# Halved low-part probability products, joined tile-0 scores, split low weight steps and a new rank table in a two-layer hybrid decoder kernel

## The chip, the cores and the metric

The kernel runs on one core of a Trainium2 chip. TensorE (PE) multiplies, VectorE (DVE), ScalarE (ACT) and GpSimd (POOL) do the elementwise work, and SyncE (SP) issues most DMAs. The metric is the device time of one execution in microseconds; smaller is better. Of the kernel before, three timed runs gave 553.5, 553.61 and 555.03 us (median 553.61).

## The reference

The input is 512 tokens of width 1024; two layers follow each other, then a final RMSNorm. In each layer one projection gives the columns of four mixers that work side by side:

```python
h = rmsnorm(x, norm_w)
p = split_cols(h @ w_in)
o_a = dsa_mixer(...)       # ReLU indexer over 8 heads -> top-k keys per query -> softmax attention, 4 heads
o_b = nsa_mixer(...)       # compressed, selected and window branches, each a softmax, sigmoid-gated and added
o_c = shortconv_mixer(...) # 3-wide causal convolution between two gates
o_d = pool_mixer(...)      # causal means over 2/4/8/16 tokens, a small linear map
mixed = concat(silu(gate) * o for each group)
x = x + mixed @ w_out
```

In the indexer, `score = sum_h relu(qi_h . ki) * wi_h`. In each attention, scores go through an exponential, are divided by their row sum, and are multiplied with the values; in mixer B the result is also multiplied by a gate per head and branch. With 512 tokens every block of the selected branch is admissible, so it and the window branch are both plain causal attention, each with its own keys and values.

## The kernel before, in words

Float32 accuracy is had from two fp32r operands: a number is split into a high part (`wh`, `ph`, `hT[0]`, ...) and a low part (`wl`, `pl`, `hT[1]`, ...), and a product is the sum of high*high, high*low and low*high matmuls.

The 512 tokens are four tiles of 128. A layer is: normalisation and transposition of the tiles into `hT`; the projections (token-major ones in `group_a`, `group_idx`, `group_bk`, `group_bq`; channel-major ones by `lin_ch`, with 512 columns a step); the compression of keys and values (`compress`, `compressed`); attention A and B for each tile (`att_a`, `att_b`); convolution and pooling; and the output projection (`out_tile`).

Weights come in parts of 256 rows (`load_w`, line 566). A part is loaded by SP into `st` (four buffers), ACT writes its high part `wh`, and POOL the low part `wl = st - wh`, one subtraction over both 128-row halves `k` of the part. A buffer `st` comes free when `wl` is done. In the first group (`start=True`) DVE makes `wh`, and POOL and DVE take turns with `wl`. `compressed` (line 965) also uses the `st` buffers, for the compression weights, and multiplies them in 64 small matmuls; each is two instructions in a trace.

The indexer (`group_idx`, line 800) does, for tiles 1 to 3 and eight heads each: a matmul into a PSUM bank `s` (there are two), a ReLU by ACT into the SBUF tile `rl` (two buffers), and `acc = rl * wi + acc` by DVE. `topk` then takes the largest values out of `acc` on DVE.

`probs` (line 1005) does for each of the four heads: two matmuls (high and low keys) into a bank `s`; a DVE operation that adds the mask and finds the minimum `mn`; the exponential on ACT into `pb` with the row sum `rs`. Then DVE takes the reciprocal of `rs`, multiplies it with the gate in mixer B (`rs<-rs,gt`), and POOL scales `pb`. `pv` (line 1039) handles 128 keys at a time: four transposes of `pb` into a bank `tr`, the high part `ph` by ACT, the low part `pl` by DVE, and two matmuls with all 512 columns into the bank `pv`. The value operand `vt(k)` has 128 columns: 64 of the high part of V and 64 of the low part; `finish` adds the two halves.

All engines' orders are made before the program runs. Every operation is recorded on a `Tape` (line 521 issues each, so every instruction of a trace has line 521 and rows are told apart by their tiles). `schedule` lists them with a table of costs (`cost`, line 318): on each engine, of the operations that could start within 1 ns of the soonest, the one with the lowest rank goes first. The ranks are the table `RANK`, one number for each recorded stage. `warm` records 40 transposes of the identity that nothing reads.

```python
PE.matmul(po, vt(k), ph, start=first and k == 0, stop=False)      # pv, before
PE.matmul(po, vt(k), pl, start=False, stop=last and k == i)
S.activation(rl[:, :n], ps[:, :n], AF.Relu)                       # group_idx, before
lo(V if start and h % 2 else G, wl[:, :, :n], st[:, :, :n], wh[:, :, :n])   # load_w, before
```

Of the kernel before, what the change touches and what calls it, by code (L numbers as in the profile page):

```python
# [178 lines left out]
class Op:  # L179
    __slots__ = ("eng", "name", "args", "kw", "outs", "ins", "before", "left", "behind", "dur", "occ", "seen",  # L180
                 "tiles", "start", "ready", "num", "locks", "moves", "stage", "rank", "group", "load")


class Engine:
# [43 lines left out]
class Tape:  # L228
# [37 lines left out]
    def record(self, eng, name, args, kw):  # L266
# [11 lines left out]
        op.group = None  # L278
        op.behind = []
# [8 lines left out]
        for views, writes in ((op.ins, False), (op.outs, True)):  # L288
            for v in views:
# [3 lines left out]
                if adds:  # L293
                    op.group = v.tile.groups.setdefault((r0, r1, bits), [])
                    op.group.append(op)
                    for (a, b, _), other in v.tile.groups.items():
                        if other is not op.group and a < r1 and r0 < b:
                            op.before.update((o.num, o) for o in other)
# [19 lines left out]
    def cost(self, op):  # L318
# [9 lines left out]
        if op.name == "dma_start":  # L328
# [3 lines left out]
            op.seen = 2000 + rows * (2.1 + run / 685.0)  # L332
            if op.eng == "ACT" and not any(o.eng == "ACT" for o in self.ops):
                op.occ = 1650
# [59 lines left out]
    def schedule(self):  # L394
# [24 lines left out]
        def earliest(op):  # L419
# [4 lines left out]
            for t in op.tiles:  # L424
# [6 lines left out]
                elif pl.pool.name == "pp":  # L431
                    s = max([s] + [at for other, at in t.used.items() if other != e])
            return s
# [10 lines left out]
        while len(order) < len(ops):  # L444
# [9 lines left out]
            if e == "PE" and last[e] is not None:  # L454
                s = max(s, last[e].start + op.load * (2 if last[e].start < COLD else 1))
# [882 lines left out]
```

## Time and profile before

| what | value |
|---|---|
| median of three timed runs | 553.61 us |
| the profiled execution's own time | 555.73 us |
| its span (first to last instruction) | 554.0 us |
| PE busy | 530.8 us (96%) |
| weight loads (PEld) busy | 457.0 us (82%) |
| DVE busy | 423.3 us (76%) |
| ACT busy | 318.2 us (57%) |
| POOL busy | 297.8 us (54%) |
| DMA | 50.62 MB, mean 91 GB/s |
| mean granted TensorE clock | 0.993 |

A busy share counts an instruction from its start to its end. Matmuls overlap in the pipeline of PE, so the distance between the starts of two steps is what a step costs, not its own duration. PE is nearly always busy here, so a piece of time has to come out of PE's steps, out of the waits between them, or out of the stretches at the two ends where PE has nothing to do. Other engines matter where PE waits for what they make.

### The profile page before, as it was taken

The numbers are of one execution on the slowest core, as the hardware profiler recorded it, in microseconds if no ns is written. First come the engines' busy times: TensorE is split into PE (matmuls) and PEld (weight loads), VectorE is DVE, ScalarE is ACT, GpSimd is POOL, SyncE is SP. The second block draws the span as 40 slices with busy tenths as digits, with TensorE's granted clock in tenths as the row PEclk, the third lists the DMA queues.
The fourth block names the chain that finished last, engine by engine and source line by source line (L and its number), as shares of the span: only waits on it lengthen the run. The fifth ranks groups of instructions, "written<-read, shape, count | busy, mean of one in ns | idle before, by whom it ended". The sixth has DMA issues, their size and how long they took to land.

```text
span 554.0 us, 9676 instructions
## 1 busy us (share of the span) xinstructions
PE 530.8 (96%) x3097; PEld 457.0 (82%) x3097; DVE 423.3 (76%) x1153; ACT 318.2 (57%) x797; POOL 297.8 (54%) x398
## 2 busy tenths in 40 slices
PE   6999999999999999999999999989999999999995
PEld 6999987767887778789999899878778777888995
DVE  4648999999995787843266589998999878797733
ACT  5468855634554676754356686454555665675623
POOL 5655753653446746553665556257455567463632
PEclk9999999999999999999999999989999999999998
DMA  8861222641313111106662333147232202130304
GB/s 270 262 162 30 61 70 72 153 112 31 89 46 87 57 49 46 40 20 203 194 181 66 87 78 88 48 116 177 72 87 57 76 30 59 28 98 10 95 1 151
DMA packets 70098, 50.62 MB, mean 91 GB/s; under 512 B 19224, under 2 KB 64416, under 8 KB 70048
## 3 DMA queue, kind: packets, MB, share of 16 engines
q1 hardware_dynamic: 69888, 49.75, 32.8%
q8 instruction: 24, 0.39, 0.3%
q14 instruction: 26, 0.21, 0.1%
q10 hardware_dynamic: 160, 0.27, 0.1%
HBM read 45.81 MB, written 4.19 MB: 90 GB/s over the span
## 4 chain that ended last, share of the span: by engine, by line
PE 80%; DVE 6%; ACT 5%; DMA 3%; POOL 3%; issue 2%; SPq 0%; POOLq 0%; ACTq 0%; DVEq 0%
PE mm L521 58%; PE tr L521 10%; PE s L521 7%; PE pv L521 5%; POOL wl L521 2%; DMA st<-in_w_in_dram 1%; ACT wh L521 1%; DVE acc L521 1%; DVE pb L521 1%; DMA x<-in_x_dram 1%; DMA st<-in_w_out_dram 1%; DVE om L521 1%; POOL pb L521 1%; ACT rl L521 1%; DVE pl L521 0%
## 5 line engine op out<-in xcount | busy, mean ns | idle before, releaser
L521 POOL TENSOR_TENSOR wl<-st,wh 128x768 fp32r<-128x768 f32 (+4 forms) x94 | 160.2, 1713 | 98.4 <-ACT wh L521 87.2
L521 PE MATMUL mm<-hT,wh 128*128 128x512 f32 x544 | 178.1, 405 | 3.3 <-ACT wh L521 2.7
L521 PEld LDWEIGHTS mm<-hT,wh 128*128 128x128 f32 x544 | 100.4, 190 | 24.3 <-ACT wh L521 4.9
L521 PE MATMUL mm<-wh,hT 128*128 128x360 f32 (+3 forms) x480 | 104.8, 309 | 1.5 <-ACT z L521 0.9
L521 PE MATMUL mm<-hT,wl 128*128 128x512 f32 x272 | 103.6, 401 | 0.0
L521 PE MATMUL mm<-wh,mT 128*128 128x384 f32 (+1 forms) x384 | 92.7, 324 | 0.4 <-DVE x L521 0.4
L521 ACT ACTIVATE wh<-st 128x768 fp32r<-128x768 f32 (+4 forms) x92 | 70.8, 776 | 31.9 <-DMA st<-in_w_in_dram 14.5
L521 POOL TENSOR_SCALAR pb<-pb,rs 128x512 f32<-128x512 f32 (+3 forms) x96 | 55.7, 597 | 52.5 <-DVE rs L521 35.6
L521 PEld LDWEIGHTS mm<-wh,hT 128*128 128x128 f32 x480 | 78.5, 189 | 3.4 <-ACT z L521 1.8
L521 PEld LDWEIGHTS mm<-wh,mT 128*128 128x128 f32 x384 | 66.4, 189 | 3.6 <-ACT wh L521 1.0
L521 PE MATMUL mm<-wl,hT 128*128 128x360 f32 (+3 forms) x240 | 68.3, 306 | 0.0
L521 ACT ACTIVATE pb<-pb,mn 128x128 f32<-128x128 f32 (+3 forms) x96 | 53.5, 558 | 25.2 <-DVE mn L521 24.8
L521 PE MATMUL mm<-wl,mT 128*128 128x384 f32 (+1 forms) x192 | 59.3, 321 | 0.3 <-POOL wl L521 0.3
L521 PEld LDWEIGHTS mm<-hT,wl 128*128 128x128 f32 x272 | 51.0, 189 | 9.5 <-POOL wl L521 0.4
L521 DVE MAX8 m<-acc 128x8 f32<-128x256 f32 (+2 forms) x96 | 51.9, 551 | 0.8
L521 DVE MATCH_REPLACE8 acc<-m,acc 128x384 f32<-128x384 f32 (+2 forms) x96 | 51.8, 541 | 0.1
L521 DVE TENSOR_TENSOR pl<-tr,ph 128x512 fp32r<-128x512 f32 x60 | 40.4, 684 | 9.5 <-ACT ph L521 7.9
L521 ACT ACTIVATE ph<-tr 128x512 fp32r<-128x512 f32 (+1 forms) x68 | 38.2, 592 | 15.0 <-PE tr L521 14.7
L521 PE MATMUL tr<-ident,pb 128*128 128x128 f32 x240 | 43.3, 275 | 2.3 <-POOL pb L521 2.2
L521 PEld LDWEIGHTS mm<-wl,hT 128*128 128x128 f32 x240 | 43.4, 189 | 0.5 <-POOL wl L521 0.2
L521 DVE CUSTOM_DVE_ANT_0 pb<-s,mask 128x128 f32<-128x128 f32 (+3 forms) x72 | 33.1, 461 | 10.0 <-PE s L521 5.2
L521 PEld LDWEIGHTS tr<-ident,pb 128*128 128x128 f32 x240 | 29.9, 140 | 11.4 <-POOL pb L521 6.0
(159 smaller groups left out, 889.0 us busy)
## 6 DMA issues: line engine op xcount, KB each, us to landing
st<-in_w_in_dram SPq DMA_DIRECT2D x104, 128.0 KB, 2.5
st<-in_w_in_dram SPq DMA_DIRECT2D x28, 256.0 KB, 3.2
st<-in_w_out_dram SPq DMA_DIRECT2D x16, 384.0 KB, 3.3
x<-in_x_dram SPq DMA_DIRECT2D x16, 256.0 KB, 5.0
st<-in_w_in_dram SPq DMA_DIRECT2D x8, 320.0 KB, 3.3
st<-in_w_out_dram SPq DMA_DIRECT2D x8, 256.0 KB, 2.7
x1d<-x SPq DMA_DIRECT2D x8, 256.0 KB, 3.8
x<-x1d SPq DMA_DIRECT2D x8, 256.0 KB, 3.4
```

What stands on the lines that cost most here:

```text
L521: getattr(self.engines[op.eng].real, op.name)(*[real(a) for a in op.args], **{k: real(v) for k, v in op.kw.items()})
```

## The change

- In `pv` the low part `pl` meets only the 64 high columns of the values, in two matmuls of 256 columns each; the high part `ph` still meets 128 columns. The product of low part and low values is no longer added (except in the one step of tile 0 of mixer A).
- In mixer B, tile 0, the scores of the window branch, the selected branch and the compressed branch come out of one pair of matmuls per head (`probs_joint`, 2 x 160 columns).
- `load_w` makes `wl` in two subtractions, one for each 128-row half; in the first group POOL takes the first half and DVE the second. ACT's queue issues the first part's DMA.
- The ReLU of the indexer is written back into its PSUM bank; `rl` is gone.
- The gate is no longer multiplied into `rs` on DVE but given to POOL's scaling of `pb` as a second multiplier.
- The tape lets a matmul over a part of a region join that region's accumulation group, prices DMAs otherwise, and counts a step's weight load when it picks the next step. The table `RANK` is a new one.

```diff
 RANK = [
-    583, 29, 585, 581, 518, 0, 283, 160, 177, 3, 101, 151, 129, 145, 507, 102, 0, 68, 584, 582, 532, 0, 74, 105,
+    3, 2, 577, 31, 1, 0, 0, 41, 54, 50, 52, 46, 4, 53, 12, 19, 0, 47, 11, 51, 14, 0, 17, 60, 106, 83, 0, 100, 0,
...
-            op.seen = 2000 + rows * (2.1 + run / 685.0)
+            op.seen = 2000 + rows * (0.56 + run / 437.0)
...
+            if e == "PE" and before is not None:
+                s = max(s, before.start + op.load * (2 if before.start < COLD else 1))
             return s
...
-            if e == "PE" and last[e] is not None:
-                s = max(s, last[e].start + op.load * (2 if last[e].start < COLD else 1))
...
-                SP.dma_start(
+                (S if start and h == 0 else SP).dma_start(
                     st[:, :, o : o + c],
...
-            lo(V if start and h % 2 else G, wl[:, :, :n], st[:, :, :n], wh[:, :, :n])
+            for k in range(2):
+                lo(V if start and k else G, wl[:, k, :n], st[:, k, :n], wh[:, k, :n])
...
-                rl = wk.tile([P, T], F32, name=nm("rl"), tag="rl", bufs=2)
-                S.activation(rl[:, :n], ps[:, :n], AF.Relu)
-                V.scalar_tensor_tensor(a[:, :n], rl[:, :n], wi[i][:, h : h + 1],
+                S.activation(ps[:, :n], ps[:, :n], AF.Relu)
+                V.scalar_tensor_tensor(a[:, :n], ps[:, :n], wi[i][:, h : h + 1],
...
-            if gcol is not None:
-                V.tensor_mul(rs, rs, gate[i][:, :, gcol])
             for h in range(NH):
                 p = pb[h]
-                G.tensor_scalar(p, p, rs[:, h : h + 1], 0.0, op0=OP.mult, op1=OP.add)
+                if gcol is None:
+                    G.tensor_scalar(p, p, rs[:, h : h + 1], 0.0, op0=OP.mult, op1=OP.add)
+                else:
+                    G.tensor_scalar(p, p, rs[:, h : h + 1], gate[i][:, h, gcol : gcol + 1], op0=OP.mult, op1=OP.mult)
...
+                p3 = ps[:, 0:320].rearrange("p (b n) -> p b n", b=2)          # probs_joint, for each head
+                PE.matmul(p3, qT["b", 0][:, h, :], kTB[0][:, :, 0:160], start=True, stop=False)
+                PE.matmul(p3, qT["b", 0][:, h, :], kTB[1][:, :, 0:160], start=False, stop=True)
...
-                PE.matmul(po, vt(k), ph, start=first and k == 0, stop=False)
-                PE.matmul(po, vt(k), pl, start=False, stop=last and k == i)
+
+                end = last and k == i
+                if not end:
+                    PE.matmul(po, vt(k), ph, start=first and k == 0, stop=False)
+                if end and i == 0:
+                    PE.matmul(po, vt(k), pl, start=True, stop=False)
+                else:
+                    for c in (slice(0, T // 2), slice(T // 2, T)):
+                        PE.matmul(po[0:HD, c], vt(k)[:, 0:HD], pl[:, c], start=False, stop=False)
+                if end:
+                    PE.matmul(po, vt(k), ph, start=False, stop=True)
```

The new orders are shown at three places. The first is PE in mixer B of layer 1, where `pl` meets the values (`tr` from `pb` are the transposes, `mm` the projections). Before:

```order
L521 MATMUL mm_1738<-hT_194,wh_1648 128x512
L521 MATMUL s_1787<-kTB_941,qb_1122 128x512
L521 MATMUL s_1787<-kTB_951,qb_1122 128x512
L521 MATMUL pv_1731<-ph_1778,vB_854 128x512
L521 MATMUL pv_1731<-pl_1783,vB_854 128x512
L521 MATMUL tr_1795<-kTB_941,qb_1122 128x32
```

And now:

```order
L529 MATMUL pv_1829<-ph_2015,vB_853 128x512
L529 MATMUL pv_1829<-pl_2018,vB_853 64x256 x2
L529 MATMUL tr_2030<-ident,pb_1869 128x128
L529 MATMUL tr_2030<-ident,pb_1891 128x128
L529 MATMUL pv_1829<-pl_2023,vB_853 64x256
L529 MATMUL pv_1829<-ph_2026,vB_853 128x512
L529 MATMUL tr_2030<-ident,pb_1908 128x128
L529 MATMUL pv_1829<-pl_2023,vB_853 64x256
```

The low product is now two steps, here once in a row (`x2`) and once apart, each behind another kind of step. Of the 116 halves in the program, 56 stand right behind their other half and 15 right behind a transpose.

The second place is PE behind the small compression matmuls of layer 1 (`tr` from `st` and `u`), up to the first projections with weights (`wh_1479` before, `wh_1542` now) whose buffers the compression held. Before:

```order
L521 MATMUL tr_1406<-st_1322,u_106 32x64
L521 MATMUL mm_1452<-hT_194,wh_1114 128x512
L521 MATMUL mm_1452<-hT_212,wh_1114 128x512
L521 MATMUL mm_1452<-hT_194,wl_1156 128x512
...
L521 MATMUL mm_1452<-hT_194,wl_1309 128x512
L521 MATMUL mm_1452<-hT_194,wh_1254 128x512
L521 MATMUL mm_1452<-hT_212,wh_1254 128x512
L521 MATMUL mm_1488<-hT_194,wh_1479 128x512
```

And now:

```order
L529 MATMUL tr_1466<-st_1353,u_152 32x64
L529 MATMUL s_1508<-kTB_98,qb_1310 128x512
L529 MATMUL s_1508<-kTB_104,qb_1310 128x512
L529 MATMUL tr_1518<-ident,pet_901 128x16
L529 MATMUL s_1528<-kTB_98,qb_1310 128x512
L529 MATMUL s_1528<-kTB_104,qb_1310 128x512
L529 MATMUL tr_1547<-ident,zc_1515 128x32
L529 MATMUL mm_1552<-hT_255,wh_1542 128x512
```

Twelve projection and score steps stood between the two before; now four score steps and two small transposes do. In layer 2 it went the other way: two score steps and six transposes stood there before, and eleven projection steps and one transpose do now.

The third place is DVE at the start of the program (`st` are the weight parts, `xn` normalised tiles, `hT` the low part of the transposed ones). Before:

```order
L521 COPY g_col<-tr_125 128x8
L521 SCALAR_TENSOR_TENSOR xn_164<-x_81,ss_133,s_141 128x512
L521 SCALAR_TENSOR_TENSOR xn_174<-x_85,ss_133,s_157 128x512
L521 CAST wh_188<-st_102 128x2x360
L521 SCALAR_TENSOR_TENSOR xn_199<-x_92,ss_155,s_141 128x512
L521 TENSOR_TENSOR hT_212<-tr_181,hT_194 128x4x128
```

And now:

```order
L529 COPY g_col<-tr_122 128x8
L529 CAST wh_168<-st_90 128x2x360
L529 TENSOR_TENSOR wl_175<-st_90,wh_168 128x360
L529 CAST wh_186<-st_102 128x2x360
L529 TENSOR_TENSOR wl_216<-st_102,wh_186 128x360
L529 SCALAR_TENSOR_TENSOR xn_232<-x_81,ss_163,s_139 128x512
L529 SCALAR_TENSOR_TENSOR xn_238<-x_92,ss_163,s_154 128x512
L529 CAST wh_263<-st_165 128x2x360
L529 TENSOR_TENSOR hT_273<-tr_240,hT_255 128x4x128
```

Three weight parts are now cast ahead of the first tile's low part, and the first two ahead of the tile's normalisation. All 40 unread transposes now stand ahead of the first tile's own; before, they were spread between its steps and those of the next tiles.

## Rows read from the trace of the kernel before

**Rows 1.** The page's first part: busy time, share of the span, instructions.

```profile
PE 530.8 (96%) x3097; PEld 457.0 (82%) x3097; DVE 423.3 (76%) x1153; ACT 318.2 (57%) x797; POOL 297.8 (54%) x398
```

**Rows 2.** Timeline, PE near 137 us: start us, us, engine, operation, tiles, shapes, count.

```profile
137.16 0.40 PE L521 MATMUL mm<-hT,wl 128*128 128x512 f32 x1
137.40 0.39 PE L521 MATMUL mm<-hT,wh 128*128 128x512 f32 x1
137.63 0.39 PE L521 MATMUL pv<-pl,vB 128*128 128x512 f32 x1
137.86 0.60 PE L521 MATMUL tr<-ident,es 128*96 128x128 f32 x4
```

**Rows 3.** Waits of the weight loads: total us, times, longest us.

```profile
PEld mm L521 <- ACT wh L521: 6.4, 13, 1.7
PEld tr L521 <- POOL pb L521: 6.0, 13, 1.4
PEld s L521 <- DVE mn L521: 4.6, 10, 1.1
PEld s L521 <- ACT rl L521: 3.3, 9, 1.0
PEld mm L521 <- POOL wl L521: 1.8, 5, 0.7
```

**Rows 4.** Timeline, PE in the output projection: 256-column steps.

```profile
538.04 0.28 PE L521 MATMUL mm<-wl,mT 128*128 128x256 f32 x1
538.16 0.40 PE L521 MATMUL mm<-wh,mT 128*128 128x256 f32 x2
538.40 0.28 PE L521 MATMUL mm<-wl,mT 128*128 128x256 f32 x1
```

**Rows 5.** Timeline, PE near 462 us: four transposes with 128-column weights.

```profile
462.44 0.60 PE L521 MATMUL tr<-ident,pb 128*128 128x128 f32 x4
```

**Rows 6.** Timeline, weight loads of two 160-column score steps.

```profile
179.80 0.30 PEld L521 LDWEIGHTS s<-kTB,qb 128*128 128x128 f32 x2
```

**Rows 7.** Groups of DVE by form: count | busy us, mean ns | idle before.

```profile
L521 DVE SCALAR_TENSOR_TENSOR acc<-rl,wi,acc 128x512 f32<-128x512 f32 x14 | 13.4, 958 | 0.5 <-ACT rl L521 0.4
L521 DVE SCALAR_TENSOR_TENSOR acc<-rl,wi,acc 128x256 f32<-128x256 f32 x14 | 10.0, 718 | 1.3 <-ACT rl L521 1.1
L521 DVE TENSOR_TENSOR rs<-rs,gt 128x4 f32<-128x4 f32 x16 | 8.6, 537 | 0.1
L521 DVE TENSOR_TENSOR x<-mm,x 128x256 f32<-128x256 f32 x16 | 6.8, 422 | 14.5 <-PE mm L521 14.4
L521 DVE SCALAR_TENSOR_TENSOR cd<-cd,mm 128x512 f32<-128x512 f32 x8 | 5.5, 683 | 2.3 <-ACT cd L521 2.3
```

**Rows 8.** Groups of ACT and POOL by form.

```profile
L521 ACT ACTIVATE rl<-s 128x512 f32<-128x512 f32 x16 | 9.5, 596 | 7.4 <-DVE acc L521 6.9 <-PE s L521 0.2
L521 POOL TENSOR_TENSOR wl<-st,wh 128x768 fp32r<-128x768 f32 x56 | 104.5, 1872 | 65.7 <-ACT wh L521 55.2 <-PE s L521 6.9 <-DMA st<-in_w_in_dram 1.9
L521 POOL TENSOR_TENSOR wl<-st,wh 128x512 fp32r<-128x512 f32 x20 | 26.7, 1349 | 21.7 <-ACT wh L521 21.7
```

**Rows 9.** Timeline, PE around the compressions of layer 1 and layer 2.

```profile
92.09 0.41 PE L521 MATMUL tr<-st,u 128*32 128x64 f32 x8
...
94.85 0.61 PE L521 MATMUL mm<-hT,wh 128*128 128x512 f32 x2
95.76 0.74 PE L521 MATMUL mm<-hT,wh 128*128 128x512 f32 x2 [0.29 <-ACT wh L521]
...
363.85 2.17 PE L521 MATMUL tr<-st,u 128*32 128x64 f32 x64
...
367.27 0.49 PE L521 MATMUL s<-kiT,qiT 96*128 96x512 f32 x1
369.11 2.36 PE L521 MATMUL mm<-hT,wh 128*128 128x512 f32 x5 [1.34 <-ACT wh L521]
```

**Rows 10.** Windows: PE, PEld, DVE, ACT, POOL busy us (instructions), PEclk, DMA share, GB/s.

```profile
370.00:374.00 4.00, 4.00 (x13) 3.19 (x12) 3.86 (x9) 2.01 (x5) 4.00 (x4) 0.66 0.63 148
```

**Rows 11.** Timeline, DVE at the start: the third weight part's cast.

```profile
16.19 0.53 DVE L521 CAST wh<-st 128x720 fp32r<-128x720 f32 x1
```

More of the change, by code (lines that the diff above doesn't have):

```diff
@@ L180 @@
     __slots__ = ("eng", "name", "args", "kw", "outs", "ins", "before", "left", "behind", "dur", "occ", "seen",
-                 "tiles", "start", "ready", "num", "locks", "moves", "stage", "rank", "group", "load")
+                 "tiles", "start", "ready", "num", "locks", "moves", "stage", "rank", "group", "load", "part")
 class Engine:
@@ L278, in record @@
         op.group = None
+        op.part = False
         op.behind = []
@@ L293, in record @@
                 if adds:
-                    op.group = v.tile.groups.setdefault((r0, r1, bits), [])
+                    for (a, b, had), other in v.tile.groups.items():
+                        if a == r0 and r1 < b and bits & ~had == 0:
+                            op.group = other
+                            op.before[other[0].num] = other[0]
+                            op.part = True
+                    if op.group is None:
+                        op.group = v.tile.groups.setdefault((r0, r1, bits), [])
+                        if kw["stop"]:
+                            op.before.update((o.num, o) for o in op.group if o.part)
                     op.group.append(op)
@@ L331, in cost @@
             op.dur = op.occ = 480
-            op.seen = 2000 + rows * (2.1 + run / 685.0)
-            if op.eng == "ACT" and not any(o.eng == "ACT" for o in self.ops):
-                op.occ = 1650
+            op.seen = 2000 + rows * (0.56 + run / 437.0)
+            if op.eng == "ACT" and sum(o.eng == "ACT" for o in self.ops) == 2:
+                op.occ += 1280
         elif op.eng == "PE":
@@ L938, in layer @@
         kcT = [kTB[s][:, 1, 0:32] for s in range(2)]
+        for s in range(2):
+            G.memset(f(kTB[s][:, 0, 0:32]), 0.0)
         vc = res.tile([96, P], F32R, name=nm("vc"), tag="vc")
@@ L1031, in probs, with probs_joint, head, weigh @@
             V.reciprocal(rs, rs)
-            if gcol is not None:
-                V.tensor_mul(rs, rs, gate[i][:, :, gcol])
             for h in range(NH):
                 p = pb[h]
-                G.tensor_scalar(p, p, rs[:, h : h + 1], 0.0, op0=OP.mult, op1=OP.add)
+                if gcol is None:
+                    G.tensor_scalar(p, p, rs[:, h : h + 1], 0.0, op0=OP.mult, op1=OP.add)
+                else:
+                    G.tensor_scalar(p, p, rs[:, h : h + 1], gate[i][:, h, gcol : gcol + 1], op0=OP.mult, op1=OP.mult)
+            return pb
+        @tape.staged
+        def probs_joint(cmp):
+            pb = [[], []]
+            mn, rs = ([sm.tile([P, NH], F32, name=nm("mn"), tag=t) for _ in range(2)] for t in ("mn", "rs"))
+            for b in range(2):
+                big = [wk.tile([P, 2, T // 2], F32, name=nm("pb"), tag="big", bufs=BIG) for _ in range(2)]
+                pb[b] = [big[h // 2][:, h % 2, :P] for h in range(NH)]
+            @tape.staged
+            def head(h):
+                ps = bank("s", 2)
+                p3 = ps[:, 0:320].rearrange("p (b n) -> p b n", b=2)
+                PE.matmul(p3, qT["b", 0][:, h, :], kTB[0][:, :, 0:160], start=True, stop=False)
+                PE.matmul(p3, qT["b", 0][:, h, :], kTB[1][:, :, 0:160], start=False, stop=True)
+                cmp(h, p3[:, 1, 0:32])
+                for b in (1, 0):
+                    p = pb[b][h]
+                    V.tensor_tensor_reduce(out=p, in0=p3[:, b, 32:160], in1=mask[:, T - P :], scale=-0.125, scalar=3.0e38,
+                                           op0=OP.add, op1=OP.min, accum_out=mn[b][:, h : h + 1])
+                    S.activation(p, p, AF.Exp, scale=-1.0, bias=mn[b][:, h : h + 1], accum_out=rs[b][:, h : h + 1])
+            @tape.staged
+            def weigh(b):
+                V.tensor_scalar(rs[b], rs[b], 1.0e-30, None, op0=OP.max)
+                V.reciprocal(rs[b], rs[b])
+                for h in range(NH):
+                    G.tensor_scalar(pb[b][h], pb[b][h], rs[b][:, h : h + 1], gate[0][:, h, 1 + b : 2 + b], op0=OP.mult,
+                                    op1=OP.mult)
+            for h in range(NH):
+                head(h)
+            weigh(1)
+            weigh(0)
             return pb
@@ L1086, in att_b @@
             po = bank("pv", 1)
+            if i == 0:
+                pb = probs_joint(cmp)
+                pv(po, pb[1], i, lambda k: vB[:, k, 1, :], True, False)
+                cmp_probs(i, e, mx)
+                pv(po, pb[0], i, lambda k: vB[:, k, 0, :], False, False)
+                cmp_pv(i, e, es, po)
+                finish("b", i, po, 2)
+                return
             joint = 32 + n <= T
```

53 rows, old and new, of the table RANK are left out of this document.

## The prediction

> **What bounds the kernel now.** I read the busy shares first. PE is busy for 530.8 of 554.0 us, DVE for 423.3, POOL for 297.8 [rows 1]. The shares alone don't say what a PE step costs, so the timeline comes next: steps of 512 columns start 0.23 us apart (137.16, 137.40, 137.63, 137.86) although each is drawn 0.39 long [rows 2]. PE is the bound, and by its steps. What can be won beside shorter steps is the time between them, so the third view is the waits of the weight loads. Five kinds make up most of it: 6.4 us on ACT for high weights, 6.0 on POOL for scaled probabilities, 4.6 on DVE's minimum `mn`, 3.3 on ACT's ReLU and 1.8 on POOL for low weights [rows 3]. That is 22.1 us, in many pieces of 0.1 to 1.7 us. A gain of more than 2% would need nearly all of it, so I expect a small one.
>
> **The parts and their prices.**
>
> *Two half steps for `pl`.* There are 60 low steps; 58 become 116 halves and two stay. A full step costs 0.23 us [rows 2]. 256-column steps start 0.12 us apart (three of them between 538.04 and 538.40) [rows 4]. So 58 x 0.23 = 13.3 us become 116 x 0.12 = 13.9: +0.6 us. Fewer weight columns don't shorten a step whose 256 columns pass anyway. They could help only where the step before is shorter than a weight load, behind a transpose. Four transposes whose weights have 96 columns take 0.60 us, and so do four with 128 columns [rows 2, 5]: a transpose lasts (0.60 - 0.27)/3 = 0.11 us whatever loads next, 0.27 being the drawn length of the last one. I count nothing for it.
>
> The Trainium skill, "TensorE: Matmul & The Clock Gate", section "LDWEIGHTS (loading the stationary operand)", says that a load's time grows with its columns, columns/1.2 ns; that gives 107 ns for 128, 80 for 96 and 53 for 64 (an estimate from that page). If this set the spacing, a transpose followed by a 64-column load would fall from 0.11 to about 0.06 us: 0.75 us at the 15 places of the new order, 5.8 if all 116 halves stood so. This case's trace speaks against that: the 96- and the 128-column transposes take the same 0.60 us.
>
> *Joined scores of tile 0.* Per layer 4 heads x 2 steps x 2 branches, with 160 and 128 columns, become 8 steps of 320. Two loads of 160-column steps take 0.30 us together; with one load's length of 0.19 taken off, they stand 0.11 apart [rows 6], and 128 columns can't be dearer. A 320-column step lies between 0.12 (256) and 0.23 (512): 0.147 by interpolation. In both layers 32 x 0.11 = 3.5 becomes 16 x 0.147 = 2.4: -1.2 us. PE's steps together: -0.6 us.
>
> *DVE.* With the ReLU's result in PSUM the indexer's addition has one SBUF operand less. Its mean is 958 ns at 512 columns; a like operation with an operand in PSUM takes 683; at 256 columns 718 stands against 422 [rows 7]. At 0.28 us each, 48 of them save 13 us. The 16 products `rs<-rs,gt` go: 4 numbers a row, yet 537 ns each, 8.6 us. DVE loses about 22 of 423 us, and the part it loses lies in the chains that PE waits for: `mn` stands behind the indexer's additions in DVE's queue, and `rs` ahead of the scaled probabilities. Of the 4.6 + 3.3 us of waits on `mn` and on the ReLU [rows 3] I take half, -4.0; all of it is -7.9. The other end is a loss. Before, a PSUM bank is free once ACT has read it (0.60 us, [rows 8]); now it stays held through DVE's addition, some 0.7 us more, and the two `rl` buffers that let ACT run ahead of DVE are gone. ACT already waited 6.9 us for `acc` at 512 columns alone [rows 8]. That ACT writes into PSUM, no row shows; I take 0.60 us again, and between 0.4 and 0.8 it stays under cover, since ACT is busy for 57% [rows 1].
>
> *Low weights in halves.* 768 columns take 1872 ns and 512 take 1349: 2.04 ns a column and 0.30 us fixed [rows 8]. A half of 384 takes 1.09, so the first half is ready 0.78 us sooner, the second 0.30 later, and POOL works 102 x 0.30 = 31 us more (298 to 329 of 554). Of the 1.8 us of waits for low weights I take -1.0 (ends -1.8 and +1.0). For the scaled probabilities two things work against each other: no `rs<-rs,gt` ahead of 64 of the 96 scalings and shorter POOL operations to queue behind, but 31 us more in that queue. PE waits 6.0 us here; I take -1.5 (ends -6.0 and +4.0). Buffers `st` come free 0.3 us later per part, and SP's loads queue behind that; in most places they are early by more.
>
> *The new order at the compressions.* The next weights can be loaded only when the compression gives its buffers back. In layer 1 the small steps end at 92.50, and the first step with those weights starts at 95.76, 3.3 us on; twelve steps lie between, and PE stands for about 0.6 us (94.85 and two steps of 0.23 make 95.31, then 0.45 to the start and a load of 0.1) [rows 9]. In layer 2 the same path took 366.02 to 369.11, and PE stood for about 1.7 us of it (367.27 and one step make 367.50, then 1.6 and a load of 0.1) [rows 9]. The path is set by a DMA and a cast, not by PE. Now layer 1 has 4 x 0.23 + 2 x 0.11 = 1.1 us of PE work there, so it stands for about 2.2 us, 1.6 more than before. Layer 2 has 11 x 0.23 + 0.11 = 2.6 us, so it stands for about 0.5, 1.2 less: +0.4 together. Behind layer 2's stop the granted clock averaged 0.66 over 370 to 374 us [rows 10], after 2.2 us of small steps and a wait; the clock was at the lower of its two levels (1.2 of 2.4 GHz) for 0.34/0.5 = 68% of that stretch, which costs 4 x 0.34 = 1.4 us. Layer 1 had no such drop. The new order can move it to layer 1; I count its cost once, as before (ends -1.4 and +1.4).
>
> *The start.* Before, the third weight part lies behind ten x halves, two parts and a gain row, 3.99 MB, and is cast at 16.19 [rows 11], so at least 0.28 MB/us after some 2 us. Now 2.95 MB lie up to it: 12.5 us at the latest, 13.0 with its cast. PE's fifth step of the first tile needs it, and DVE makes the tile's low part only behind it; the order before could begin on other parts. From there on nothing is missing any more. I take +0.5 us (ends -1.5 and +2).
>
> *All other places* change order too, by the table; the sum gives them nothing either way, but they are why its range is wide.
>
> **Sum.** -0.6 - 4.0 - 1.0 - 1.5 + 0.4 + 0.5 = -6.2 us. The profiled execution took 555.73 us for its span of 554.0, so 549.5; its own time is 2.1 above the median of the timed runs, 553.61, which the same step brings to 547.4. If this is what happens, 544.5 to 550.5 holds it.
>
> **Rivals.**
>
> *More of the waits go.* DVE's relief and the order reach the waits on POOL and ACT as well, and half of the remaining 22.1 - 6.5 = 15.6 us goes: 6.2 + 7.8 = 14 us, 539.6. For it: DVE is the second busiest engine [rows 1] and every chain passes it. Against it: 6.4 us are weights that wait for DMA and buffers, which nothing here shortens, and POOL gets longer. Chance 0.15.
>
> *The waits only move.* PE's steps hardly change (-0.6), and a wait that goes at one place turns up at another, as at the two compressions. 552 to 555, say 553. For it: PE's steps carry 96% of the span. Chance 0.17.
>
> *The held banks, on the slower side.* In the indexer DVE runs late, PE and ACT can now be only two steps ahead of it instead of four, and PE's next score step waits for DVE's addition. There are 48 such steps. If each is late by 0.25 us, 48 x 0.25 = 12 us are lost against the 6 won: 559.4. It decides from about 0.13 us a step, where the two are equal. For it: ACT's waits on `acc` [rows 8]. Against it: the new order puts a score step of the indexer mostly 1.2 to 2.5 us apart in PE's work, and ACT plus DVE need about 1.3 us at 512 columns, with two banks. Chance 0.18.
>
> **How the numbers follow.** Forecast 0.50, more 0.15, moved 0.17, held banks 0.18. The likeliest gives 547.4. Below 541.5 lies about 0.08 (most of the second case's lower half), above 557 about 0.11 (the far part of the last), so the range is 541.5 to 557. A measurement of this kernel tells about 0.3% (1.7 us) from no change: faster is below 551.9, slower above 555.3. Faster: 0.49 + 0.15 + 0.03 = 0.67; same: 0.01 + 0.11 + 0.02 = 0.14; slower: 0.03 + 0.16 = 0.19.
>
> **What would show it.** The halves: starts 0.12 us apart, and a transpose ahead of one still 0.11 long (0.06 would prove the load rule). The joined scores: 0.147 us a step. DVE: additions of 0.68 us at 512 columns, DVE's total near 401 us, and waits on `mn` and the ReLU near 4 us instead of 7.9; if waits on `acc` stand ahead of `s` steps instead, the held banks are right. POOL: low halves of 1.09 us and a total near 329. Compressions: a stop of about 2.2 us in layer 1 and 0.5 in layer 2, with the clock's drop at one of them or none. Start: the third part's cast near 12.5 us. I am wrong if the five kinds of waits together stay above 20 us, or fall below 10.

## The result, and the profile after

The changed kernel took 548.07 us (median of four runs, 547.27 to 548.37); the kernel before took 554.0 in the same job. The ratio is 0.9888, with a 95% interval of 0.9869 to 0.9907. The forecast was 547.4. The time is right; the account behind it is right only in part, and the rows below already show where.

The first part of the page after, as [rows 1]:

```profile
PE 528.5 (97%) x3139; PEld 455.9 (83%) x3139; DVE 403.9 (74%) x1139; ACT 320.7 (59%) x797; POOL 320.4 (59%) x504
```

The span of the profiled execution fell from 554.0 to 546.4. PE is busy for 2.3 us less, and idle for 5.3 us less (554.0 - 530.8 = 23.2, now 17.9). DVE lost 19 us, POOL gained 23.

The same stretch of PE as in [rows 2] doesn't exist any more. These are three others of the new order: two half steps (from 165.74 to the next step at 165.97), a half step behind a transpose (the weight loads, from 149.93 to 150.04), and two joined score steps.

```profile
165.51 0.39 PE L529 MATMUL mm<-hT,wl 128*128 128x512 f32 x1
165.74 0.39 PE L529 MATMUL pv<-pl,vA 128*64 128x256 f32 x2
165.97 0.63 PE L529 MATMUL mm<-hT,wh 128*128 128x512 f32 x2
...
469.83 0.46 PE L529 MATMUL s<-kTB,qb 128*128 128x320 f32 x2
```

```profile
149.71 0.14 PEld L529 LDWEIGHTS tr<-ident,pb 128*128 128x128 f32 x1
149.93 0.14 PEld L529 LDWEIGHTS pv<-pl,vB 128*64 128x64 f32 x1
150.04 0.14 PEld L529 LDWEIGHTS tr<-ident,pb 128*128 128x128 f32 x1
```

A pair of halves takes 0.23 us, as one full step did. The load after a half's load comes 0.11 us later: the transpose that runs meanwhile lasts as long as ever, and a load of 64 columns instead of 128 saves nothing. Two joined steps are drawn 0.46 long and a single one 0.31 (mean of the 16: 309 ns), so they stand 0.15 apart.

The waits of the weight loads, as [rows 3] (total us, times, longest):

```profile
PEld mm L529 <- ACT wh L529: 8.8, 14, 2.3
PEld s L529 <- DVE acc L529: 5.2, 21, 0.5
PEld tr L529 <- POOL pb L529: 4.8, 15, 0.7
PEld mm L529 <- POOL wl L529: 2.1, 7, 0.5
PEld tr L529 <- DVE xn L529: 1.8, 2, 1.5
PEld s L529 <- DVE mn L529: 1.6, 4, 0.8
PEld tr L529 <- POOL ident L529: 1.6, 1, 1.6
...
PEld pv L529 <- ACT ph L529: 0.9, 5, 0.2
```

The waits on `mn` fell from 4.6 to 1.6. Those on the ReLU are gone, and 21 waits of score steps on DVE's `acc` stand in their place: 5.2 us for 3.3. High weights cost 2.4 us more. The five kinds together made 22.1 us and make 22.5. What fell is in kinds that the prediction left out; these are rows of before that [rows 3] doesn't hold:

```profile
PEld tr L521 <- POOL ident L521: 3.9, 1, 3.9
PEld pv L521 <- ACT ph L521: 3.6, 15, 0.4
...
PEld mm L521 <- ACT z L521: 1.8, 5, 0.7
PEld mm L521 <- ACT cd L521: 1.6, 5, 0.5
PEld pv L521 <- DVE pl L521: 1.5, 3, 0.9
```

Groups after, by form, as [rows 7, 8] (count | busy us, mean ns | idle before):

```profile
L529 DVE SCALAR_TENSOR_TENSOR acc<-s,wi,acc 128x512 f32<-128x512 f32 x14 | 10.4, 745 | 0.1
L529 DVE SCALAR_TENSOR_TENSOR acc<-s,wi,acc 128x256 f32<-128x256 f32 x14 | 6.8, 482 | 2.3 <-ACT s L529 1.9
L529 ACT ACTIVATE s<-s 128x512 f32<-128x512 f32 x16 | 9.3, 583 | 8.7 <-PE s L529 8.5
L529 POOL TENSOR_TENSOR wl<-st,wh 128x384 fp32r<-128x384 f32 x112 | 112.9, 1035 | 42.7 <-ACT wh L529 40.4 <-PE mm L529 2.0
L529 POOL TENSOR_SCALAR pb<-pb,rs,gt 128x512 f32<-128x512 f32 x16 | 14.3, 908 | 5.9 <-DVE rs L529 4.9 <-PE mm L529 1.0
```

At the compressions [rows 9, 10], PE in layer 1 and the window in layer 2:

```profile
102.97 0.74 PE L529 MATMUL s<-kTB,qb 128*128 128x512 f32 x2 [0.66 <-DVE mn L529]
104.24 0.21 PE L529 MATMUL tr<-ident,zc 32*128 32x32 f32 x1 [0.53 <-DVE zc L529]
104.38 0.50 PE L529 MATMUL mm<-hT,wh 128*128 128x512 f32 x1
```

```profile
362.00:364.00 2.00, 1.91 (x9) 1.25 (x8) 2.00 (x9) 1.26 (x2) 2.00 (x4) 1.00 0.35 80
364.00:366.00 2.00, 2.00 (x10) 1.64 (x9) 2.00 (x8) 0.00 (x0) 0.94 (x2) 1.00 0.94 240
```

In layer 1 PE now stands twice before the first step with the new weights, for 0.66 and 0.53 us, but for `mn` and for the compressed key `zc` and not for the weights. In layer 2 it stands for 0.09 us of these two windows, and the granted clock (the last but two column) stays at 1.00. Before, it averaged 0.66 in the 4 us behind this place.

The cast of [rows 11] came at 12.54:

```profile
12.54 0.54 DVE L529 CAST wh<-st 128x720 fp32r<-128x720 f32 x1 [0.56 <-DMA st<-in_w_in_dram]
```

### The profile page after: what moved, and what is told of

It is laid out like the page before. It is cut to its first block, busy times and chain, and to the rows that moved or that the text cites. A ratio compares the mean times of both kernels' runs of the same rounds, so it can differ in the third digit from the quotient of the medians.

```text
span 546.4 us, 9871 instructions
## 1 busy us (share of the span) xinstructions
PE 528.5 (97%) x3139; PEld 455.9 (83%) x3139; DVE 403.9 (74%) x1139; ACT 320.7 (59%) x797; POOL 320.4 (59%) x504
## 4 chain that ended last, share of the span: by engine, by line
PE 73%; DVE 9%; DMA 6%; ACT 4%; issue 3%; POOL 3%; SPq 1%; ACTq 0%; POOLq 0%; DVEq 0%
PE mm L529 53%; PE tr L529 8%; PE s L529 6%; PE pv L529 5%; DVE acc L529 4%; DMA st<-in_w_in_dram 3%; ACT wh L529 2%; DVE m L529 2%; POOL pb L529 1%; DMA ws<-in_w_in_dram 1%; POOL wl L529 1%; SPq L529 1%; DMA st<-in_w_out_dram 1%; ACT qiT L529 1%; DVE qb L529 1%
## 5 line engine op out<-in xcount | busy, mean ns | idle before, releaser
L529 POOL TENSOR_TENSOR wl<-st,wh 128x384 fp32r<-128x384 f32 (+4 forms) x188 | 173.5, 952 | 84.3 <-ACT wh L529 69.2
L529 PE MATMUL mm<-hT,wh 128*128 128x512 f32 x544 | 182.2, 403 | 1.4 <-ACT wh L529 1.1
L529 PE MATMUL mm<-wh,hT 128*128 128x360 f32 (+3 forms) x480 | 107.0, 308 | 3.0 <-ACT wh L529 2.9
L529 PE MATMUL mm<-hT,wl 128*128 128x512 f32 x272 | 106.8, 403 | 0.0
L529 PE MATMUL mm<-wl,hT 128*128 128x360 f32 (+3 forms) x240 | 70.4, 306 | 0.0
L529 ACT ACTIVATE pb<-pb,mn 128x512 f32<-128x512 f32 (+3 forms) x96 | 53.3, 557 | 15.1 <-DVE mn L529 14.4
L529 POOL TENSOR_SCALAR pb<-pb,rs,gt 128x512 f32<-128x512 f32 (+2 forms) x48 | 38.8, 824 | 25.8 <-DVE rs L529 12.2
L529 ACT ACTIVATE ph<-tr 128x512 fp32r<-128x512 f32 (+1 forms) x68 | 38.1, 595 | 23.2 <-PE tr L529 21.1
L529 DVE MAX8 m<-acc 128x8 f32<-128x384 f32 (+2 forms) x96 | 51.2, 549 | 0.3
L529 PE MATMUL tr<-ident,pb 128*128 128x128 f32 x240 | 45.7, 275 | 0.9 <-POOL pb L529 0.8
L529 DVE TENSOR_TENSOR x<-mm,x 128x256 f32<-128x256 f32 (+2 forms) x32 | 12.7, 421 | 40.8 <-PE mm L529 40.0
```

The lines of the kernel that those rows point to most:

```text
L529: getattr(self.engines[op.eng].real, op.name)(*[real(a) for a in op.args], **{k: real(v) for k, v in op.kw.items()})
```

## The experiments

Twelve kernels ran. In all but one (the old table) the order of work was kept: the list that the planner had made stayed as it was, and only the named instructions were exchanged or moved when it was written out. So a difference is that of the edit in a fixed order. The kernel before, timed beside each, took 554.0 to 555.2 us from job to job, so the ratios are what to compare.

| kernel | us | ratio to before | 95% |
|---|---|---|---|
| after | 548.07 | 0.9888 | 0.9869 to 0.9907 |
| before's order, four edits | 571.14 | 1.0292 | 1.0269 to 1.0316 |
| before's order, ReLU in PSUM alone | 572.66 | 1.0318 | 1.0286 to 1.0349 |
| before's order, the three others | 553.61 | 0.9975 | 0.9954 to 0.9996 |
| after's edits, before's table | 593.84 | 1.0689 | 1.0654 to 1.0724 |
| after, three edits undone | 562.78 | 1.0136 | 1.0113 to 1.0158 |
| after, whole low weights | 561.58 | 1.0113 | 1.0087 to 1.0139 |
| after, gate on DVE | 550.09 | 0.9908 | 0.9883 to 0.9932 |
| after, full low steps | 548.16 | 0.9871 | 0.985 to 0.9892 |
| after, DVE's relief put back | 558.84 | 1.0065 | 1.0042 to 1.0087 |
| after, additions over half the columns | 546.91 | 0.9863 | 0.9837 to 0.9888 |
| after, two loads moved up | 547.69 | 0.9858 | 0.9831 to 0.9884 |
| the same, and two edits more | 546.87 | 0.9845 | 0.9817 to 0.9873 |

**Edits without the order, and the table without the edits.** In the order of before, four edits were put in:

```diff
-PE.matmul(po, vt(k), pl, ...)
+for c in halves: PE.matmul(po[0:HD, c], vt(k)[:, 0:HD], pl[:, c], ...)
-S.activation(rl, ps, AF.Relu);  V.scalar_tensor_tensor(a, rl, wi, a, ...)
+S.activation(ps, ps, AF.Relu);  V.scalar_tensor_tensor(a, ps, wi, a, ...)
-V.tensor_mul(rs, rs, gate);     G.tensor_scalar(p, p, rs, 0.0, mult, add)
+                                G.tensor_scalar(p, p, rs, gate, mult, mult)
-lo(G, wl, st, wh)
+for k in range(2): lo(G, wl[:, k], st[:, k], wh[:, k])
```

> The kernel before with its own order of work, instruction by instruction, and four edits put into it: the low step as two half steps, the ReLU left in PSUM, the gate multiplied on POOL, the low weights subtracted in two halves. Joined scores and the new table are left out. Theory 1 (the edits earn it, as the prediction's sum has it): -4.0 - 1.5 - 1.0 + 0.6 = -5.9, so about 548. Theory 2 (the new order earns it, and the edits only fit into it): the waits that fall away come back as waits for banks and for POOL, 552 to 556.

571.14 us: neither theory. By themselves the edits cost 16 us. The wait that grew is the one the prediction had named as a rival:

```profile
PEld s L525 <- DVE acc L815: 24.3, 34, 2.1
```

The other way round, after's code was planned anew with the old table:

```diff
-RANK = [3, 2, 577, 31, 1, 0, 0, 41, ...]
+RANK = [583, 29, 585, 581, 518, 0, 283, 160, ...]   # stage by stage
```

> The kernel after with all its edits, but each stage gets the place that the table before gave it (the joined scores that of the first of the two branches, their second weighing that of the other). Theory 1 (edits): 546 to 549, no worse than after. Theory 2 (order): at least 552, and the stops that after has lost stand in it again.

593.84 us. The old table belongs to another list of operations and other costs, and with the edits in it gives a far worse order. This run mixes the planner's new costs with the old table, so it says how much the order matters, and not why.

**The ReLU alone, and the three others without it.** Of the diff above, the second pair of lines alone, in before's order:

> The kernel before in its own order, with only the ReLU left in PSUM. Held banks: the score steps of the indexer wait for DVE's additions as they did with four edits (24 us in 34 places), 566 to 572. DVE's relief (the prediction's -4.0): 549 to 551, if the loss of the kernel with four edits comes from one of the other three.

572.66 us. DVE's total fell from 423.3 to 411.6 us, and yet score steps wait for its additions as long as with four edits, so the loss is the held bank's:

```profile
PEld s L525 <- DVE acc L808: 24.0, 33, 2.1
```

Then the other three pairs of lines without it:

> The kernel before in its own order with three edits and without the fourth: half steps, the gate on POOL, low weights in two halves; the ReLU's result goes to SBUF as before. From the two kernels with the ReLU in PSUM (571.1 with the three, 572.7 without) they are worth 1.5 us: 553.5. By the prediction's terms (+0.6 - 1.0 - 1.5) 553.1, and about 551 with the products that DVE no longer does. If they need the new order as the ReLU does, 556 or more.

553.61 us, 0.9975: about 1.4 us won (0.2 to 2.6 by the interval), as the difference of the other two runs had said. The prediction's three terms for them make -1.9. The waits on `mn` fell from 4.6 to 3.5 us and those on `pl` from 1.5 to 0.5. Those for scaled probabilities rose, from 6.0 to 6.7 us (the two `pb` lines), and `ph`, `z` and `cd` stayed as they were in the kernel before:

```profile
PEld tr L525 <- POOL pb L1016: 5.1, 10, 1.8
...
PEld pv L525 <- ACT ph L525: 3.6, 14, 0.4
...
PEld mm L525 <- ACT z L525: 1.9, 5, 0.7
PEld tr L525 <- POOL pb L525: 1.6, 2, 1.0
...
PEld mm L525 <- ACT cd L525: 1.5, 4, 0.5
```

**Why the bank costs so much in the old order.** The prediction counted on two banks `s`. The trace of before shows that the indexer has one. PE writes a score step of an attention head at 36.69, and DVE reads it only after the top-k, at 142.69:

```profile
36.69 0.28 PE L521 MATMUL s<-kTA,qa 128*128 128x256 f32 x1
```

```profile
142.69 0.42 DVE L521 CUSTOM_DVE_ANT_0 pb<-s,acc 128x256 f32<-128x256 f32 x1 [0.38 <-PE tr L521]
```

One of the two banks is taken for 106 us, all of the indexer of layer 1. By the planner's list of banks, 46 of the 48 score steps of before are followed on their own bank by the next one. In the trace, 42 of the 48 next users of the bank start (with their weight load) before DVE's addition has ended, by 42 us in all; that was free while ACT's ReLU released the bank. In the new order, where they have to wait for the addition, 32 steps of 48 have the next one behind them on the same bank: layer 1 is held in the same way (41.97 to 150.53), in layer 2 the steps use both. Between 40 and 110 us, in layer 1, the waits on `acc` are 12.4 us with the ReLU edit alone in the old order and 2.7 in the new one, with one bank in either. So the new order gains by where it puts the steps, and not by a second bank.

**After's order, edits undone.** First three at once:

```diff
-for c in halves: PE.matmul(po[0:HD, c], vt(k)[:, 0:HD], pl[:, c], ...)
+PE.matmul(po, vt(k), pl, ...)
-G.tensor_scalar(p, p, rs, gate, mult, mult)
+V.tensor_mul(rs, rs, gate);  G.tensor_scalar(p, p, rs, 0.0, mult, add)
-for k in range(2): lo(G, wl[:, k], st[:, k], wh[:, k])
+lo(G, wl, st, wh)
```

> The kernel after with its own order, and three edits undone in place: one low step of 512 columns again, the gate multiplied on DVE again, whole low weights again. Theory 1: gate and low weights are worth -1.0 and about -3 of the sum, the halves +0.6, so 548.1 + 3.4 = 551.5. Theory 2: 547 to 549, and DVE longer by some 8 us without PE waiting for it.

562.78 us, far beyond both. Then one by one (the low weights of the first group, where DVE takes part, stay as they are). Full low steps (the first pair of lines):

> The kernel after with its own order and only the half steps undone: 58 low steps of 512 columns and 128 weight columns. By the prediction's price of the steps 0.6 us less, 547.5. If fewer weight columns did help (transposes ahead of them or the load itself), 549 or more. If what a longer step takes is hidden in a wait, 548.

548.16 us: no difference that can be measured. By median it is 0.1 us more than after, by ratio 0.9 less, and the intervals overlap, so the price of 0.6 us is neither confirmed nor refuted. Whole low weights (the third pair):

> The kernel after in its own order, with only the low weights subtracted whole again (one POOL instruction of 768 columns for two of 384). The prediction counted the halves as worth 1.0 us, so 549. By the trace of the kernel with three edits undone, whose weight loads waited 14.4 us for low weights instead of 2.1, most of that kernel's loss is this edit alone: 557 to 562.

561.58 us. It is nearly all of the loss of the three:

```profile
PEld mm L533 <- POOL wl L609: 14.4, 23, 1.1
...
PEld tr L533 <- POOL pb L533: 5.2, 17, 0.7
```

The waits for low weights go from 2.1 to 14.4 us, in 23 places of about 0.6. When POOL makes both halves at once, the first comes 0.84 us later (1.87 for 1.035). The gate on DVE (the second pair):

> The kernel after in its own order, with only the gate multiplied on DVE again (16 small products more on DVE, and one scalar instead of two in the scaling on POOL). If the small products stand in the chain that PE waits for, 550 to 552. If the scaling with two scalars costs POOL what DVE saves, 547.5 to 549: DVE longer by 8.6 us, POOL shorter, and the waits for scaled probabilities no longer than 5 us.

550.09 us, between the two expectations and by ratio 1.1 us above after, though the intervals overlap. The waits for scaled probabilities are 4.7 us, no more than in after (4.8), as the second theory had it:

```profile
PEld tr L533 <- POOL pb L1026: 2.9, 7, 0.7
...
PEld tr L533 <- POOL pb L533: 1.8, 6, 0.7
```

The 16 products cost DVE 3.3 us here and not 8.6, and POOL's scaling is 0.1 us shorter:

```profile
L1021 DVE TENSOR_TENSOR rs<-rs,gt 128x4 f32<-128x4 f32 x12 | 2.6, 218 | 0.4
...
L1021 DVE TENSOR_TENSOR mn<-mn,gt 128x4 f32<-128x4 f32 x4 | 0.7, 174 | 0.1
```

```profile
L1026 POOL TENSOR_SCALAR pb<-pb,rs 128x512 f32<-128x512 f32 x16 | 12.7, 807 | 6.8 <-DVE rs L1021 6.8
```

**DVE's relief, put back and taken further.** An instruction of no use behind each addition:

```diff
 V.scalar_tensor_tensor(a, ps, wi, a, ...)
+V.tensor_mul(spare, mask[:, 0:128], mask[:, 128:256])
```

> The kernel after in its own order, with DVE's relief in the indexer put back: behind each of the 48 additions DVE multiplies 128 columns of the mask into a tile that nobody reads, some 0.25 to 0.3 us each, 12 to 14 us in all. If the relief is worth what the prediction says (about 4 us), 552 or more. If DVE has time to spare there, 549 or less. If each of the 21 waits for a bank grows by the whole 0.25 us, 5 us more: 553.

558.84 us, by ratio 9.8 more than after (0.0177 x 554). The new instructions took 378 ns each and not 0.25 to 0.3, 18.2 us in all:

```profile
PEld s L533 <- DVE acc L848: 14.5, 30, 1.2
```

The waits of score steps for the bank are 9.3 us longer than in after. That is most of the loss; the span of this one execution is 13.1 us longer, 3.3 more than the ratio says. Then the other way:

```diff
-V.scalar_tensor_tensor(a[:, :n], ps[:, :n], wi, a[:, :n], ...)
+V.scalar_tensor_tensor(a[:, :n//2], ps[:, :n//2], wi, a[:, :n//2], ...)   # heads 1 to 7
```

> The kernel after in its own order, with DVE relieved further: from the second head on the indexer's addition covers half of the columns only (the other half of seven heads is left out of the indexer's scores), so 42 additions fall from 0.75, 0.61 and 0.48 us to about 0.48, 0.40 and 0.35: some 8 us less on DVE. Putting 13 us of DVE's work back cost 10.8. If each us of DVE counts the same in both directions, 6 us go: 542. If only the 5.2 us of waits for banks can still go, and what is late next takes part of them, 544 to 546. If PE's order is spent, 547.5 to 548.5.

546.91 us, by ratio 1.4 less than after, within the error of both. (The kernel leaves half of the additions of seven heads out, so it shows a time and is no version to use.) The waits on `acc` fell to 0.5 us, and DVE to 396.9. In the profiled run part of the gain is lost at the start, which the edit doesn't touch: the first tile's transposes waited 2.7 us for `xn`, and the granted clock averaged 0.57 in the 4 us behind, where after had waited 1.3 us and had 1.00 throughout:

```profile
11.78 1.77 PE L533 MATMUL tr<-ident,xn 128*128 128x128 f32 x8 [2.73 <-DVE xn L533]
```

```profile
12.00:16.00 4.00, 4.00 (x18) 3.66 (x17) 3.39 (x6) 2.72 (x8) 3.82 (x9) 0.57 1.03 348
```

How often the timed runs met this stays open. What more relief is worth is therefore not settled: 1.4 us by ratio, with nothing still inside the error, and at most some 4 by an estimate from the waits (the 4.7 that went from `acc` less the new ones on POOL, `wl` 2.1 to 3.4, make 3.4).

**What is late next.** The longest stops of after are for high weights: as drawn, 2.1 us at 39.1, 0.8 at 33.0 and 1.1 at 124.2 (the expectations count each some 0.3 longer). The first two wait for loads that SP issues behind tiles needed 200 us later.

```diff
+# SP: ws part 3 and part 4 right behind part 2 (were behind pet, g and four tiles of x)
```

> The kernel after in its own order, but the third and fourth load of the indexer's weights issued right behind the second on SP, ahead of the constants, the gain row and the tiles of x that the end of the layer needs. After stops for 1.1 us at 33.0 and 2.4 us at 39.1 for the casts of these parts. If the loads alone are late, up to 3.5 us go: 544.6 to 546. If PE then waits for the next thing in that stage (ACT and DVE behind the rotary part), 547 to 548.

547.69 us: the stops at 33 and 39 are gone, and one of 2.04 us as drawn stands at 35.15, for the end of the rotary part on POOL. A wait moved. What is left, 1.7 us by ratio and 0.4 by median, can't be told from nothing, since the intervals overlap.

```profile
35.15 0.55 PE L534 MATMUL tr<-ident,z 128*128 128x128 f32 x3 [2.04 <-POOL z L534]
```

```diff
+# POOL: the last addition of the rotary part ahead of the first two low weights
-for c0, c in segs: SP.dma_start(st[:, :, o : o + c], ...)            # 3 per part
+for k in range(2): SP.dma_start(st[:, k] as 3 x 128, src[k][:, ::2, :])   # 2 per part
```

> The kernel with the two weight loads moved up (547.7), and two more edits. On POOL the addition that ends the rotary part of the third tile runs ahead of the first two low weights instead of behind them: PE waited 2.3 us for it at 35, and it comes 1.4 us earlier. The weight parts of three pieces are loaded with two instructions on SP instead of three: in 111 to 122 us SP issued 17 without a pause, and PE then stood for 1.4 us at 124. If both stops go by that much, 545 to 545.5. If the casts or POOL are late next, 546.5 to 547.7.

546.87 us, ratio 0.9845: the shortest of all, though its interval still touches that of after. The stop at 35 fell to 0.6 us on PE and another of 0.9 for low weights came behind it; that at 124 fell by 0.2. It is the version to keep, with a gain over after of about 0.4% by ratio and 0.2% by median.

## Why the prediction was right, point by point

**PE's steps, -0.6.** Right. Halves cost 0.23 a pair and joined steps 0.15; PE's busy time fell by 2.3 us, and the clock's drop that is in the one profile and not in the other makes 1.4 of it, by the prediction's working from [rows 10]. That fewer weight columns would not shorten a transpose held: 0.11 us ahead of a 64-column load. The Trainium skill ("TensorE: Matmul & The Clock Gate", "LDWEIGHTS (loading the stationary operand)") prices the load alone, by its columns; an estimate from that page, with the load setting the spacing, was 0.06. Here the load does not set it.

**DVE, -4.0.** DVE's total was right (403.9 us against 401), the account was not. The additions gave less than priced: 0.745 us against 0.68 at 512 columns, and 42 of the 48 together 34.2 us before and 25.7 after, where 48 were to save 13. ACT's ReLU into PSUM took 0.58 us at 512 columns, as assumed (0.60). The step said that of 4.6 + 3.3 us of waits half would go. They are 1.6 + 5.2: -1.1. The shorter additions do carry much, since putting 18 us of DVE's work back costs 9.8; but what they carry is the held bank's cost, which the edit itself had brought. The new order with the ReLU back in SBUF was not run, so whether this edit earns anything there stays open.

**The held banks.** This rival, given 0.18, was no rival but half of the mechanism. Its price was 0.25 us a step; in the old order it is 24 us / 48 = 0.5, in the new 5.2 / 48 = 0.11, just below the 0.13 from which it was to decide. What failed is the argument against it: "with two banks" was wrong, one is held by an attention head through the indexer. The new order makes up for most of it by where it puts the steps.

**Low weights in halves, -1.0.** The waits didn't fall (1.8 to 2.1), so as a term of a sum against before it is wrong by about a microsecond. As an edit in the new order it is worth 12.5 us (0.0225 x 554). Both are true: the new order has PE use low weights earlier than the old one did, and can do so only because the first half is there 0.8 us sooner (1.035 us against 1.872).

**Scaled probabilities, -1.5.** 6.0 to 4.8: -1.2. The number was right, the reasons were not. They were that the gate's product goes and that POOL's operations get shorter. With both in the old order the waits rose, to 6.7 us (6.9 with the ReLU in PSUM as well); in the new order they are 4.7 with the gate back on DVE, 5.2 with whole low weights and 4.9 with both and full low steps. So the fall came with the new order and not with these edits, and that the term fits is luck. That the scaling itself would get longer by 0.1 us through its second factor was not foreseen.

**Compressions, +0.4, and the clock.** 1.2 us of stop in layer 1 (2.2 forecast, and for other reasons) and 0.1 in layer 2 (0.5); against the 0.6 and 1.7 of before that is -1.0 where +0.4 was forecast. The clock's drop is in neither place in the profile of after, which is the end of -1.4 that the prediction named. But the drop does not belong to the order. In the profiled run of the three edits, in before's order, the granted clock stayed at 1.00 behind layer 2's compressions and was lower at 226 us instead:

```profile
226.00:230.00 4.00, 4.00 (x15) 2.92 (x16) 2.67 (x7) 2.09 (x4) 2.81 (x5) 0.57 0.01 4
370.00:374.00 4.00, 4.00 (x18) 3.03 (x18) 3.80 (x11) 1.83 (x4) 4.00 (x6) 1.00 0.70 159
```

With full low steps, in after's order, it averaged 0.59 over 38 to 42 us, where after had 1.00. The mean granted clock of the timed runs of all jobs lies between 0.990 and 0.999 for before, and between 0.993 and 0.997 for after. So the -1.4 is a difference of two single executions, and no run shows it as a part of the gain between the medians.

**The start, +0.5.** The third cast came at 12.54 (12.5 forecast), and PE waited 1.3 us for `xn` ahead of the first tile, where it had waited 0.9 for `hT`. The first projection step began 3.2 us later than before:

```profile
9.57 0.59 PE L521 MATMUL mm<-wh,hT 128*128 128x360 f32 x2
```

```profile
12.72 0.43 PE L529 MATMUL mm<-wh,hT 128*128 128x360 f32 x1
```

This was made up soon: the last of the 96 steps of 360 columns of layer 1 starts at 31.84, before at 31.86.

**All other places, 0.** Here the sum failed. The prediction called its five kinds of waits "most of it"; they were 22.1 of 45.3 us, less than half. They stand at 22.5 us now, above the 20 that was to show the prediction wrong. All waits of the loads fell from 45.3 to 39.0: what went is 2.7 on `ph`, 1.6 on `z`, 1.4 on `cd`, 1.3 on `pl` and 2.3 on the start's `ident`, less what came. The last is no gain, since unread transposes took its place. `ph`, `z` and `cd` stood unchanged in the old order with three edits, so their fall is the new order's; `pl` had fallen there from 1.5 to 0.5, so most of that is the edits'. Three terms were too favourable by some 6 us together: DVE 2.9, low weights 1.3, and high weights 2.0, which rose by 2.4 where only the compressions' 0.4 was counted. What gave this back is in part the `ph`, `z` and `cd` of the new order; the rest is not accounted for term by term. The number was met partly by luck. What the runs do show is that neither side earns the gain alone: in the old order four of the edits cost 16 us, and the new order without three of them is 7.5 us slower than before (0.0136 x 555). The joined scores, the first group's halves and ACT's DMA were not run apart, so what each earns stays open.

## What to carry to other kernels

An edit and the order of work are priced together: the ReLU's edit cost 17.6 us in the order that was not planned for it, and undoing the halved low weights cost 12.5 in the order that was planned with them. Before an operand is left in PSUM, look in the trace for who else holds the banks, from the step that writes one to the instruction that reads it, since a count of banks in the code says nothing of how many are free. And test the sum against the waits by kind, not against the time alone.

## What the runs showed of the hardware

In one and the same order of work, DVE's small instructions with two operands in SBUF follow the length of POOL's. The same 4-column product and 64-column difference, in after and with whole low weights on POOL (1.87 us instead of 1.04 each):

```profile
L529 DVE TENSOR_TENSOR kk<-zk,kk 128x64 fp32r<-128x64 f32 x8 | 2.9, 364 | 2.4 <-ACT kk L529 2.2
L529 DVE TENSOR_TENSOR mx<-mx,gt 128x4 f32<-128x4 f32 x8 | 2.2, 273 | 0.0
```

```profile
L533 DVE TENSOR_TENSOR kk<-zk,kk 128x64 fp32r<-128x64 f32 x8 | 4.9, 618 | 2.3 <-ACT kk L533 2.2
L533 DVE TENSOR_TENSOR mx<-mx,gt 128x4 f32<-128x4 f32 x8 | 3.7, 458 | 0.0
```

DVE's total rose from 403.9 to 413.0 us in that kernel without an instruction more. The 537 ns of `rs<-rs,gt` in [rows 7], which were 218 in the kernel with the gate on DVE and shorter subtractions on POOL, fit this; where an instruction stands beside POOL's matters as well, since `mx<-mx,gt` took only 286 ns in the kernel before, beside long ones too.

The indexer's addition shows the same from the other side. With the ReLU's result in SBUF it took 958 ns at 512 columns in the kernel before, and 909 in the same order with halved low weights on POOL. With it in PSUM, so with one operand less in SBUF, it took 745 in after, 746 there with whole low weights on POOL and 748 in the old order with whole ones: POOL's length no longer shows.

The Trainium skill has a rule for this ("SBUF — State Buffer", "SBUF: two separate sides"): DVE and GpSimd share a pair of ports, for which a DVE instruction with two SBUF inputs competes, and whichever takes it first keeps it for its whole instruction. These rows agree; that the ports are what DVE waits for, none of them shows by itself.

POOL's scaling with a second factor from memory takes 908 ns at 512 columns, with a constant 807.
